# Ten input chunks of a decoder layer's mixer as five pairs with seven block products, and the memory-key projection placed behind the output projection

## The chip, the cores and the metric

The kernel runs on one core of a Trainium2 chip. The metric is the device time of one execution in microseconds (us); the median of three runs of the kernel before is 1890.21 us (1889.72 to 1892.38). The engines are named as the profile names them: PE is TensorE (matmuls), PEld its weight loads, DVE is VectorE, ACT is ScalarE, POOL is GpSimd, and SP issues most of the DMAs. Each engine works through its own instructions in the order in which the built program lists them.

## The reference, cut to what matters

One decoder layer on 256 tokens of width 2048, in float32: a SwiGLU half-step, a mixer, cross-attention into 256 memory tokens, and a second SwiGLU half-step. The change is in the mixer and at the start of the cross-attention.

```python
def hybrid_mixer(h, pos, w_in, ...):
    proj = h @ w_in                       # 2048 -> 6144 + 16 columns
    qa, ka, va, qg, kg, vg, rg, glr = jnp.split(proj, splits, axis=-1)
    qa = rope(rms_norm(heads(qa, 8), attn_q_norm), pos) * (HEAD_DIM ** -0.5)
    ka = rope(rms_norm(heads(ka, 8), attn_k_norm), pos)
    o_attn = dilated_attention(qa, ka, heads(va, 8))
    ...                                   # gated linear attention of qg, kg, vg, glr, gated by silu(rg)
    return jnp.concatenate([o_attn, o_gla], axis=-1) @ w_out

def cross_attention(h, m, ...):
    k = rms_norm((m @ w_k).reshape(...), k_norm)   # m: normed memory tokens
    ...
```

## The kernel before, in words

**Exact products from split operands.** Every float32 operand is split into a high part (a cast) and the rest (operand less high part), and a product is three matmuls: high by high, high by rest, rest by high. The weights are split on the fly. A weight tile `raw` of 128 x 4 x 512 (four k tiles of 128 rows, 512 columns, 1 MB) is loaded by one DMA and split in two halves: ACT casts `wh` (128 x 1024; L157 in `wgroup`, L204 in `parts`) and DVE subtracts for `wl` (L158, L205). There are four buffers each for `wh` and `wl` (`WB`), so a half can be split only when PE is done with an earlier one. The activations lie transposed and split in `xT[0..3]`, four k tiles by 256 tokens each.

**The mixer.** `w_in` has 12 chunks of 512 columns. `proj` takes one chunk: two PSUM banks (one for each block of 128 tokens, t = 0 and 1), four groups of four k tiles, and for each half of a group 12 matmuls of 128x512 (2 token blocks x 2 k tiles x 3), in all 96. The pool `pa` has four banks, so that a chunk's two banks are read while the next chunk fills the other two. The chunks come in the order 6, 7 (queries and keys of the gated linear attention), 8, 9 (its values), 10, 11 (its gates), 0, 2, 1, 3 (attention queries and keys of two head groups), 4, 5 (attention values).

**What follows a chunk** is small work between the splits. For queries and keys (`roped`, L810) it is, for each token block: squares on ACT (L520), their sum on DVE (L522), two small scalings (L525, L526), a power on POOL (L400), the factor on DVE (L530), four scaled copies `un` out of the bank on ACT (L817), and the rotation by a product on POOL (L821), two on DVE (L825) and a sum (L827). Until the last `un` of a token block the bank is held. Turns onto PE (transposes, `scores`, `probs_turn`, `attend`) are put off with `later(n, ...)` by n ticks; a `proj` ticks once for each half of a group. `scores` has, for each of four heads in a group, two reductions with mask (L855), exponentials on ACT (L856), products with counts (L857) and a reciprocal (L860).

**Seven block products.** The two SwiGLU steps already use `seven` (L288): where two column blocks and two groups of four k tiles meet two token blocks, eight products of 128 x 512 x 512 are replaced by seven, with sums of weight tiles and differences of activation blocks (class `Blocks`). A sum of weight tiles is made by DVE (`add`, L211, 128x2048) or by a DMA that POOL issues and that adds into the tile (`add_hbm`, L218). A `product` is 12 matmuls from two halves, so a half feeds six matmuls there; `plain` is the ordinary product for two token blocks and feeds 12 from a half.

**Order.** A list scheduler orders each engine's instructions by priorities (`WPRI`, `LPRI`, `FPRI`) and by its own estimate of when each is ready; pools give out buffers in that order. After the attention values the memory keys are projected (`xattn_w_k`, L967), then the output projection `w_out` runs (L974), then the cross-attention queries.

Of the kernel before, what the change touches and what calls it, by code (L numbers as in the profile page):

```python
# [32 lines left out]
PR0 = 10  # L33
PR1 = 9
ATT = 4
# [5 lines left out]
XPRI = 170  # L41
MEM0 = 2
MEMS = 3
UF = 20
UM = 36
SB = 6
RF = 9
RM = 5


@with_exitstack
def layer_kernel(ctx: ExitStack, tc: tile.TileContext, A: dict, out: bass.AP):
# [48 lines left out]
    def later(n, fn):  # L101
        pend.append([n, fn])
# [67 lines left out]
    def proj(W, c, lhs, groups, fine=None, mid=None):  # L170


        n = W.shape[-1]
        acc = [pa.tile([P, n], F32, tag="acc", name="acc") for _ in range(TT)]
        groups = list(groups)
        for i, g in enumerate(groups):
            if fine and i:
                fine(4 * i)
            if mid and i == 2:
                mid()  # L180
# [107 lines left out]
    def seven(F, ld, rest, hbm):  # L288
# [52 lines left out]
        return Y, Z, R if rest else sv, X  # L341

    def split_from_psum(hi, lo, ps):
        SC.copy(hi, ps)  # L344
        V.tensor_sub(lo, ps, hi.bitcast(F32))  # L345
# [48 lines left out]
    def lhs_x(k, t):  # L394
        hi, lo = xT[k // 4]
        sl = slice(t * P, (t + 1) * P)
        return hi[:, k % 4, sl], lo[:, k % 4, sl]

    def rpow(dst, src):
        G.tensor_tensor(dst, src, mhalf[:, :src.shape[1]], op=ALU.pow)  # L400
# [15 lines left out]
    def ffn(pre, r, after, fine=None, last=False):  # L416
# [3 lines left out]
        def turn(f, hs):  # L420
            for t in range(TT):
# [7 lines left out]
                hT[f, t] = (hi, lo)  # L429

        def x_block(t, c):
            return tuple(p[:, :, t * P:(t + 1) * P] for p in xT[c])

# [35 lines left out]
        for f in range(NF):  # L469
# [34 lines left out]
            if f == 0:  # L504
                up = proj(wu, f, lhs_x, range(4), mid=lambda: F[0].make("22-21", "12-21", "22-12"))
                fill(0, True)
# [111 lines left out]

    def gated(which, c):
        acc = proj(win, c, lhs_x, range(4))  # L620
# [18 lines left out]
    q_turn = gated("q", 6)  # L639

# [45 lines left out]
    later(7, q_turn)  # L686
    k_turn = gated("k", 7)

# [72 lines left out]

    for p2 in range(2):
        acc = proj(win, 8 + p2, lhs_x, range(4))
        for t in range(TT):
            SC.activation(vg[p2][t], acc[t], AF.Copy, scale=r2[:, t:t + 1])
        later(1, lambda p2=p2: states(p2))
        later(3, lambda p2=p2: outputs(p2))

# [12 lines left out]

    for p2 in range(2):
        acc = proj(win, 10 + p2, lhs_x, range(4))
        o2s = []
        for t in range(TT):
# [9 lines left out]
            o2s.append(o2)  # L795
        later(2, lambda p2=p2, o2s=o2s: gate_turn(p2, o2s))

# [11 lines left out]

    def roped(which, g, i, c):  # L810
        acc = proj(win, c, lhs_x, range(4))
        qns = []
# [73 lines left out]

    def values(g):
        acc = proj(win, 4 + g, lhs_x, range(4))
# [12 lines left out]

    roped("q", 0, 0, 0)
    roped("k", 0, 1, 2)
    later(ROPE + SCD, lambda: scores(0, 0))
    later(ROPE + SCD + SCI, lambda: scores(0, 2))
    roped("q", 1, 0, 1)
    later(PR0, lambda: probs_turn(0))
    roped("k", 1, 1, 3)
    later(ROPE + SCD, lambda: scores(1, 0))
    later(ROPE + SCD + SCI, lambda: scores(1, 2))  # L910

# [26 lines left out]
    for c in range(NC):  # L938
        later(MEM0 + MEMS * c, lambda c=c: mem_chunk(c))
    values(0)  # L940
    later(PR1, lambda: probs_turn(1))
    values(1)
    for c in range(NC):
        later(1 + c, lambda c=c: mem_sq(c))

# [20 lines left out]

    acc = proj(A["xattn_w_k"], 0, lhs_mem, range(4))  # L967
    rm = rstd_of(ssm, "rm")
    rmsq = squared(rm, "rmsq")
    heads_T(acc, rm, rmsq, "k", 81, XK)  # L970


    ss3 = new_ss("ss3")
    for c in range(NC):  # L974
        acc = proj(A["w_out"], c, lhs_m, (2, 3, 0, 1))
        for t in range(TT):
            V.tensor_add(xs[c][:, t], acc[t], xs[c][:, t])
        norm_chunk(c, xs[c], 32, ss3)
    r3 = rstd_of(ss3, "r3")
    r3sq = squared(r3, "r3sq")  # L980
# [168 lines left out]
```

## Time and profile before

| | |
|---|---|
| median of 3 runs | 1890.21 us |
| the profiled execution | 1891.93 us, its span (first to last instruction) 1890.2 us |
| mean granted TensorE clock | 0.998 |
| busy in the span: PE, DVE, ACT, POOL | 99%, 81%, 71%, 5% |
| chunks 8 to 5 (five later pairs) | 748.4 to 998.0 us of the span |
| DMA | 433.02 MB, mean 229 GB/s |

The span starts at the first instruction. The timeline gives for each instruction its start, its length and, in brackets, the idle time of its engine before it with what ended it. Instructions of one engine overlap a little (the next starts before the last one's length is over), so what an instruction costs in a row of equal ones is the distance of starts. The stages named below are cut at the times at which ACT starts to read a chunk's bank.

### The profile page before, as it was taken

To read this page: it belongs to the slowest core of one execution; us is meant where nothing else is said; L and a number is where in the kernel's file an instruction comes from. 1 tells how busy PE (TensorE), PEld (TensorE's weight loads), DVE (VectorE), ACT (ScalarE), POOL (GpSimd) and SP (SyncE) were. 2 spreads that over 40 slices of the span, in tenths; PEclk is the share of its full clock that TensorE was granted. 3 is DMA by queue.
4 is the path that set the end of the run, shared out by engine and by line. 5 is a ranking of instruction groups with operands and counts; after the bars stand their busy time and mean duration, and the time that the engine had idled before them with its cause. 6 is when DMAs were issued, how large, how long until landed. Compare 5 with 4: busy or idle time off the path is not lost.

```text
span 1890.2 us, 22717 instructions
## 1 busy us (share of the span) xinstructions
PE 1875.2 (99%) x8552; PEld 1547.0 (82%) x8552; DVE 1527.1 (81%) x1521; ACT 1349.7 (71%) x1785; POOL 90.5 (5%) x103
## 2 busy tenths in 40 slices
PE   9999999999999999999999999999999999999999
PEld 7887888888888888778888889788788888888887
DVE  6989999999999965446775565687999999999994
ACT  6768788787778786445676445566778787878786
POOL 0000000000000000002210000000000000000000
PEclk9999999999999999999999999999999999999999
DMA  9758877987788644445465551756867987788872
GB/s 377 271 199 278 244 229 275 300 250 210 264 286 269 199 184 167 156 156 203 170 223 189 204 186 68 297 176 240 260 207 274 304 252 212 254 284 274 243 235 95
DMA packets 65755, 433.02 MB, mean 229 GB/s; under 512 B 7371, under 2 KB 8523, under 8 KB 14828
## 3 DMA queue, kind: packets, MB, share of 16 engines
q1 hardware_dynamic: 55852, 369.69, 50.8%
q0 software_dynamic: 8064, 58.72, 16.4%
q10 hardware_dynamic: 1728, 3.15, 0.5%
q8 instruction: 67, 1.10, 0.2%
q14 instruction: 44, 0.36, 0.1%
HBM read 429.44 MB, written 2.10 MB: 228 GB/s over the span
## 4 chain that ended last, share of the span: by engine, by line
PE 98%; DVE 1%; DMA 1%; ACT 0%; issue 0%; ACTq 0%
PE acc L231 13%; PE acc L230 13%; PE acc L232 13%; PE acc L167 9%; PE acc L168 9%; PE acc L166 9%; PE dn L166 8%; PE dn L168 8%; PE dn L167 8%; PE tp L426 1%; DMA raw<-in_ffn_w_gate_dram 1%; PE tp L384 0%; DVE wl L205 0%; DVE raw L211 0%; PE dsp L728 0%; PE op L745 0%
## 5 line engine op out<-in xcount | busy, mean ns | idle before, releaser
L205 DVE TENSOR_TENSOR wl<-raw,wh 128x1024 fp32r<-128x1024 f32 x548 | 649.1, 1221 | 93.1 <-ACT wh L204 91.5
L204 ACT CAST wh<-raw 128x1024 fp32r<-128x1024 f32 x548 | 566.2, 1051 | 197.3 <-PE dn L168 84.0
L158 DVE TENSOR_TENSOR wl<-raw,wh 128x1024 fp32r<-128x1024 f32 (+1 forms) x370 | 443.4, 1219 | 182.3 <-ACT wh L157 181.3
L157 ACT CAST wh<-raw 128x1024 fp32r<-128x1024 f32 (+1 forms) x370 | 382.9, 1048 | 199.6 <-PE acc L168 158.4
L166 PE MATMUL dn<-wh,hTh 128*128 128x512 f32 x704 | 274.4, 391 | 0.6 <-ACT hTh L344 0.6
L168 PE MATMUL dn<-wh,hTl 128*128 128x512 f32 x704 | 274.3, 390 | 0.0
L167 PE MATMUL dn<-wl,hTh 128*128 128x512 f32 x704 | 274.2, 389 | 0.0
L231 PE MATMUL acc<-wl,xTh 128*128 128x512 f32 x672 | 263.4, 392 | 2.6 <-DVE wl L205 2.6
L232 PE MATMUL acc<-wh,xTl 128*128 128x512 f32 x672 | 261.8, 390 | 0.0
L230 PE MATMUL acc<-wh,xTh 128*128 128x512 f32 x672 | 261.4, 389 | 0.0
L166 PE MATMUL acc<-wh,xTh 128*128 128x512 f32 x544 | 215.6, 397 | 5.2 <-ACT wh L157 5.2
L211 DVE TENSOR_TENSOR raw<-raw 128x2048 f32<-128x2048 f32 x96 | 218.1, 2286 | 2.6 <-DMA raw<-in_ffn_w_gate_dram 2.5
L167 PE MATMUL acc<-wl,xTh 128*128 128x512 f32 x544 | 213.5, 392 | 0.8 <-DVE wl L158 0.8
L168 PE MATMUL acc<-wh,xTl 128*128 128x512 f32 x544 | 213.2, 392 | 0.0
L230 PE MATMUL acc<-wh,Fh 128*128 128x512 f32 x456 | 179.9, 395 | 0.0
L231 PE MATMUL acc<-wl,Fh 128*128 128x512 f32 x456 | 178.0, 390 | 0.0
L232 PE MATMUL acc<-wh,Fl 128*128 128x512 f32 x456 | 177.6, 389 | 0.0
L166 PEld LDWEIGHTS dn<-wh,hTh 128*128 128x128 f32 x704 | 132.1, 188 | 29.3 <-ACT dn L225 1.2
L168 PEld LDWEIGHTS dn<-wh,hTl 128*128 128x128 f32 x704 | 132.2, 188 | 28.3 <-DVE hTl L345 0.9
L167 PEld LDWEIGHTS dn<-wl,hTh 128*128 128x128 f32 x704 | 132.2, 188 | 27.8 <-DVE wl L158 0.5
L231 PEld LDWEIGHTS acc<-wl,xTh 128*128 128x128 f32 x672 | 126.1, 188 | 33.7 <-DVE wl L205 7.8
L230 PEld LDWEIGHTS acc<-wh,xTh 128*128 128x128 f32 x672 | 126.1, 188 | 26.3
(281 smaller groups left out, 2146.1 us busy)
## 6 DMA issues: line engine op xcount, KB each, us to landing
raw<-in_ffn_w_up_dram SPq DMA_DIRECT2D x88, 1024.0 KB, 9.1
raw<-in_ffn_w_down_dram SPq DMA_DIRECT2D x88, 1024.0 KB, 8.9
raw<-in_ffn_w_gate_dram SPq DMA_DIRECT2D x85, 1024.0 KB, 12.9
raw<-in_ffn_w_gate_dram POOLq DMA_DIRECT2D x56, 1024.0 KB, 8.6
raw<-in_w_in_dram SPq DMA_DIRECT2D x48, 1024.0 KB, 4.8
raw<-in_w_out_dram SPq DMA_DIRECT2D x16, 1024.0 KB, 4.8
raw<-in_xattn_w_k_dram SPq DMA_DIRECT2D x4, 1024.0 KB, 5.1
raw<-in_xattn_w_q_dram SPq DMA_DIRECT2D x4, 1024.0 KB, 4.7
```

What stands on the lines that cost most here:

```text
L157: SC.copy(wh[:, d], src)
L158: splits.append(V.tensor_sub(wl[:, d], src, wh[:, d].bitcast(F32)))
L166: PE.matmul(acc[t], lh, wh, start=first and i == 0, stop=False, **kw)
L167: PE.matmul(acc[t], lh, wl, start=False, stop=False, **kw)
L168: newest[0] = PE.matmul(acc[t], ll, wh, start=False, stop=last and i == len(half) - 1, **kw)
L204: SC.copy(wh, src)
L205: splits.append(V.tensor_sub(wl, src, wh.bitcast(F32)))
L211: V.tensor_add(dst, dst, src)
L230: PE.matmul(bank, hi[:, k], wh, start=start and i == 0, stop=False, skip_group_check=True)
L231: PE.matmul(bank, hi[:, k], wl, start=False, stop=False, skip_group_check=True)
L232: PE.matmul(bank, lo[:, k], wh, start=False, stop=stop and i == len(half) - 1, skip_group_check=True)
L426: PE.transpose(tp[:, j], hs[t][:, j * P:(j + 1) * P], ident)
```

## The change

Chunks 6 and 7 stay as they are. The ten others run as five pairs (c0, c1) = (9, 8), (11, 10), (2, 0), (3, 1), (5, 4). A new generator `pair` takes k groups 0 and 1 of both chunks by seven block products, and groups 2 and 3 by `plain`. Banks Y and Z hold chunk c0's two token blocks, R and X those of c1. `both` interleaves a pair with the next one: R and X are handed out first, then Y's last product follows, then the first product of the next pair, then the rest of Y and Z. The activation differences come from a `Blocks(0)` that is made during chunk 7; two of its five are written over blocks of `xT[0]` and `xT[1]`. The pool of weight tiles grows from 5 to 7 and that of general tiles shrinks from 36 to 28. The loads, sums and splits of the memory tokens and the projection of the memory keys go behind `w_out`. `product` ticks once instead of twice.

```diff
-PR1 = 9
+PR1 = 6
-MEM0 = 2
+MEM0 = 18
-UM = 36
+UM = 28
-RM = 5
+RM = 7
...
         for h, half in enumerate(parts(raw)):
             mms(bank, form, half, start and h == 0, h == 1)
-            tick()
+        tick()
...
+    def pair(F, W, c0, c1, rest):
+        Y, Z = [pa.tile([P, 512], F32, tag="acc", name="acc") for _ in range(2)]
+        T = load(W[c0, 0])
+        add_hbm(T, W[c0, 1])
+        b21 = load(W[c0, 1])
+        yield
+        product(Y, F.A21, T, True)
+        urgent(SC.copy, Z, Y)
+        yield
+        b12 = load(W[c1, 0])
+        add(T, b12)
+        product(Y, F["12-21"], T, False)
+        sw = W2([P, 512], "sw")
+        urgent(SC.copy, sw, Y)
+        product(Z, F["22-21"], b21, False)
+        product(Y, F["21-11"], b12, False)
+        add_hbm(b12, W[c0, 0])
+        sv = W2([P, 512], "sv")
+        urgent(SC.copy, sv, Y)
+        X, R = [pa.tile([P, 512], F32, tag="acc", name="acc") for _ in range(2)]
+        b22 = load(W[c1, 1])
+        add(T, b22)
+        product(R, F.A12, T, True)
+        urgent(V.tensor_sub, X, R, sw)
+        urgent(V.tensor_sub, R, R, sv)
+        forms, g = rest[0]
+        plain((Y, Z), forms, load(W[c0, g]), (1, 0))
+        product(X, F["22-12"], b22, False)
+        for forms, g in rest:
+            plain((R, X), forms, load(W[c1, g]), (0, 1))
+        yield R, X
+        product(Y, F["11-12"], b12, False)
+        yield
+        forms, g = rest[1]
+        plain((Y, Z), forms, load(W[c0, g]), (0, 1))
+        yield Y, Z
...
+    sevens = [pair(Fx, win, c0, c1, rest) for c0, c1 in ((9, 8), (11, 10), (2, 0), (3, 1), (5, 4))]
+    def both(n, out0, out1):
+        out1(next(sevens[n]))
+        if n + 1 < len(sevens):
+            next(sevens[n + 1])
+        next(sevens[n])
+        if n + 1 < len(sevens):
+            next(sevens[n + 1])
+        out0(next(sevens[n]))
...
+    later(4, lambda: Fx.make("22-21", "12-21", "22-12"))
+    next(sevens[0])
+    k_turn = gated("k", proj(win, 7, lhs_x, range(4), mid={3: lambda: next(sevens[0])}))
...
+    both(2, lambda acc: keys(0, acc), lambda acc: queries(0, acc))
+    both(3, lambda acc: keys(1, acc), lambda acc: queries(1, acc))
...
-    acc = proj(A["xattn_w_k"], 0, lhs_mem, range(4))
-    rm = rstd_of(ssm, "rm")
-    ...
     ss3 = new_ss("ss3")
     for c in range(NC):
         acc = proj(A["w_out"], c, lhs_m, (2, 3, 0, 1))
...
+    acc = proj(A["xattn_w_k"], 0, lhs_mem, range(4))
```

How the built programs order this differs at the places where a pair ends. On DVE before, where the queries of chunk 0 leave their banks (`qs`, `qm`, `qf` are the head factors, `t2` and `qn` the rotation, `wl` the splits of the next chunk, each of which feeds 12 matmuls):

```order
L522 TENSOR_REDUCE qs_7156<-sq_7154 128x4
L525 TENSOR_SCALAR qm_7158<-qs_7156,r2sq_5807 128x4
L526 TENSOR_SCALAR qm_7158<-qm_7158 128x4
L530 TENSOR_SCALAR qf_7163<-qr_7161,r2_5792 128x4
L158 TENSOR_TENSOR wl_7255<-raw_7236,wh_7254 128x1024
L825 TENSOR_TENSOR t2_7172<-un_7165,tab_6992 128x4x64 x2
L522 TENSOR_REDUCE qs_7179<-sq_7177 128x4
L827 TENSOR_TENSOR qn_7175<-t1_7170,t2_7172 128x512
L158 TENSOR_TENSOR wl_7273<-raw_7270,wh_7272 128x1024
```

On DVE in the changed kernel, the same queries, where pair (2, 0) ends and pair (3, 1) begins (`raw_7389` is the weight sum T of pair (3, 1)):

```order
L562 TENSOR_REDUCE qs_7343<-sq_7341 128x4
L565 TENSOR_SCALAR qm_7345<-qs_7343,r2sq_5807 128x4
L566 TENSOR_SCALAR qm_7345<-qm_7345 128x4
L570 TENSOR_SCALAR qf_7350<-qr_7348,r2_5792 128x4
L205 TENSOR_TENSOR wl_7425<-raw_7389,wh_7424 128x1024
L211 TENSOR_TENSOR raw_7389<-raw_7389,raw_7515 128x2048
L205 TENSOR_TENSOR wl_7438<-raw_7435,wh_7437 128x1024
L205 TENSOR_TENSOR wl_7454<-raw_7435,wh_7453 128x1024
L205 TENSOR_TENSOR wl_7519<-raw_7389,wh_7518 128x1024
L205 TENSOR_TENSOR wl_7529<-raw_7389,wh_7528 128x1024
L882 TENSOR_TENSOR t2_7359<-un_7352,tab_7100 128x4x64
L205 TENSOR_TENSOR wl_7541<-raw_7392,wh_7540 128x1024
```

One split stood between the factor and the rotation. Now, in the rows shown, a sum of weight tiles and six splits stand behind the factor, with the first half of the rotation among them; a second sum and one more split follow before its other half, and then come the second token block's chain and the keys' chain.

On DVE before, the keys of the second head group, second token block (`ks`, `km`, `kf` as above):

```order
L158 TENSOR_TENSOR wl_7968<-raw_7965,wh_7967 128x1024
L525 TENSOR_SCALAR km_7847<-ks_7845,r2sq_5807 128x4
L526 TENSOR_SCALAR km_7847<-km_7847 128x4
L530 TENSOR_SCALAR kf_7852<-kr_7850,r2_5792 128x4
L158 TENSOR_TENSOR wl_8000<-raw_7965,wh_7999 128x1024
L825 TENSOR_TENSOR t2_7861<-un_7854,tab_6993 128x4x64 x2
L827 TENSOR_TENSOR qn_7864<-t1_7859,t2_7861 128x512
L158 TENSOR_TENSOR wl_8018<-raw_8015,wh_8017 128x1024
```

And in the changed kernel, the same keys where pair (3, 1) ends and pair (5, 4) has begun (`wl_8090` feeds pair (5, 4)'s product into R, `wl_8118` its first plain product):

```order
L562 TENSOR_REDUCE ks_7962<-sq_7960 128x4
L205 TENSOR_TENSOR wl_8090<-raw_7880,wh_8089 128x1024
L565 TENSOR_SCALAR km_7964<-ks_7962,r2sq_5807 128x4
L566 TENSOR_SCALAR km_7964<-km_7964 128x4
L570 TENSOR_SCALAR kf_7969<-kr_7967,r2_5792 128x4
L882 TENSOR_TENSOR t2_7978<-un_7971,tab_7100 128x4x64 x2
L562 TENSOR_REDUCE ks_7985<-sq_7983 128x4
L884 TENSOR_TENSOR qn_7981<-t1_7976,t2_7978 128x512
L565 TENSOR_SCALAR km_7987<-ks_7985,r2sq_5807 128x4
L566 TENSOR_SCALAR km_7987<-km_7987 128x4
L570 TENSOR_SCALAR kf_7992<-kr_7990,r2_5792 128x4
L205 TENSOR_TENSOR wl_8118<-raw_8115,wh_8117 128x1024
```

Two whole chains of head factors, with the first rotation between them, now stand between two splits that PE uses one after the other; before, a split stood within every chain.

More of the change, by code (lines that the diff above doesn't have):

```diff
@@ L616, in layer_kernel, with gated @@
     qeT, keT, kdT = per_t("qeT"), per_t("keT"), per_t("kdT")
-    def gated(which, c):
-        acc = proj(win, c, lhs_x, range(4))
+    def gated(which, acc):
         sc_ = []
@@ L780, in gate_turn, with gates @@
             mT[2 + p2, t] = (hi, lo)
-    for p2 in range(2):
-        acc = proj(win, 10 + p2, lhs_x, range(4))
+    def gates(p2, acc):
         o2s = []
@@ L795, in layer_kernel @@
             o2s.append(o2)
-        later(2, lambda p2=p2, o2s=o2s: gate_turn(p2, o2s))
+        later(2, lambda: gate_turn(p2, o2s))
+    both(1, lambda acc: gates(1, acc), lambda acc: gates(0, acc))
     gb = W2([P, 4, HD], "gb")
@@ L808, in layer_kernel, with roped @@
     pn = {}
-    def roped(which, g, i, c):
-        acc = proj(win, c, lhs_x, range(4))
+    def roped(which, g, i, acc):
         qns = []
@@ L885, in attend, with values @@
             mT[g, "h", h0] = (hi, lo)
-    def values(g):
-        acc = proj(win, 4 + g, lhs_x, range(4))
+    def values(g, acc):
         va = []
```

55 lines of the change are left out of this document (29 added, 26 removed).

## Prediction

> **What bounds the kernel now.** I read the page first: the busy shares and the chain of work that ended last.
>
> ```profile
> PE 1875.2 (99%) x8552; PEld 1547.0 (82%) x8552; DVE 1527.1 (81%) x1521; ACT 1349.7 (71%) x1785; POOL 90.5 (5%) x103
> ...
> PE 98%; DVE 1%; DMA 1%; ACT 0%; issue 0%; ACTq 0%
> ```
>
> PE carries 98% of the chain. A busy PE can hide waits, so I read next what PE itself waited for (line, releaser: us in total, times, longest).
>
> ```profile
> PE acc L166 <- ACT wh L157: 5.2, 3, 3.7
> PE acc L231 <- DVE wl L205: 2.6, 2, 1.3
> PE wps L551 <- DVE x L549: 1.1, 1, 1.1
> PE acc L167 <- DVE wl L158: 0.8, 2, 0.5
> PE dn L166 <- ACT hTh L344: 0.6, 2, 0.3
> PE tp L384 <- DVE xg L386: 0.5, 1, 0.5
> ```
>
> These are all entries: PE loses 10.8 us in the whole span. So PE's matmuls are the time, as long as the splits keep up. Third, the stages: chunks (8, 9), (10, 11), (0, 2), (1, 3), (4, 5) and, last, one round of the first SwiGLU, which runs seven block products already.
>
> ```profile
> core 0: us, PE busy (x) PEld busy (x) DVE busy (x) ACT busy (x) POOL busy (x), PEclk, DMA share, GB/s
> 748.40:802.90 54.50, 54.50 (x257) 43.63 (x256) 26.06 (x29) 24.59 (x35) 1.01 (x1) 1.00 0.48 173
> 802.90:855.00 52.10, 52.10 (x234) 41.28 (x233) 25.30 (x28) 25.21 (x36) 5.08 (x4) 1.00 0.46 163
> 855.00:899.00 44.00, 44.00 (x204) 36.58 (x203) 30.66 (x39) 21.63 (x30) 9.75 (x7) 1.00 0.58 206
> 899.00:950.00 51.00, 51.00 (x239) 42.56 (x238) 39.09 (x82) 33.57 (x62) 11.08 (x9) 1.00 0.48 168
> 950.00:998.00 48.00, 48.00 (x232) 40.39 (x231) 37.94 (x80) 34.97 (x66) 4.01 (x3) 1.00 0.59 207
> ...
> 205.00:266.00 61.00, 61.00 (x274) 50.29 (x273) 56.43 (x48) 48.53 (x59) 2.62 (x3) 1.00 0.80 259
> ```
>
> DVE is half idle in the value and gate chunks, but has 39.1 of 51 us in chunks 1 and 3. The last row will speak for the change: there DVE is busy for 56.4 of 61 us and PE still never waits.
>
> **What goes.** The pace of PE's 128x512 matmuls:
>
> ```profile
> 734.26 0.39 PE L167 MATMUL acc<-wl,xTh 128*128 128x512 f32 x1
> ...
> 743.10 0.39 PE L167 MATMUL acc<-wl,xTh 128*128 128x512 f32 x1
> ```
>
> 39 matmuls lie between these starts: 8.84 / 39 = 0.2267 us each. A pair took 2 x 96 = 192 matmuls and takes 7 x 12 + 96 = 180. Five pairs save 60, **-13.6 us**.
>
> **What comes on DVE.** A pair has 7 + 4 = 11 tiles to split instead of 8, so six more `wl`, two sums of weight tiles and two bank subtractions. The rows for these and for the small work of queries:
>
> ```profile
> 876.07 0.68 DVE L522 TENSOR_REDUCE qs<-sq 128x4 f32<-128x512 f32 x1
> 876.79 0.23 DVE L525 TENSOR_SCALAR qm<-qs,r2sq 128x4 f32<-128x4 f32 x1
> 877.05 0.17 DVE L526 TENSOR_SCALAR qm<-qm 128x4 f32<-128x4 f32 x1
> 878.35 0.23 DVE L530 TENSOR_SCALAR qf<-qr,r 128x4 f32<-128x4 f32 x1 [1.12 <-POOL qr L400]
> 878.48 1.22 DVE L158 TENSOR_TENSOR wl<-raw,wh 128x1024 fp32r<-128x1024 f32 x1
> 879.78 1.87 DVE L825 TENSOR_TENSOR t<-un,tab 128x256 f32<-128x256 f32 x2
> 881.58 0.67 DVE L522 TENSOR_REDUCE qs<-sq 128x4 f32<-128x512 f32 x1
> 882.17 0.68 DVE L827 TENSOR_TENSOR qn<-t,t 128x512 f32<-128x512 f32 x1
> 882.77 1.22 DVE L158 TENSOR_TENSOR wl<-raw,wh 128x1024 fp32r<-128x1024 f32 x1
> ...
> 889.47 3.49 DVE L158 TENSOR_TENSOR wl<-raw,wh 128x1024 fp32r<-128x1024 f32 x3
> ```
>
> ```profile
> 292.85 2.29 DVE L211 TENSOR_TENSOR raw<-raw 128x2048 f32<-128x2048 f32 x1 [0.37 <-DMA raw<-in_ffn_w_gate_dram]
> 295.06 2.35 DVE L205 TENSOR_TENSOR wl<-raw,wh 128x1024 fp32r<-128x1024 f32 x2
> ```
>
> By distance of starts: a split (3.49 - 1.22) / 2 = 1.14, a weight sum 2.21, a 128x512 sum 0.60, one token block's rotation 1.80, and its chain of head factors (876.07 to 878.48) 2.41, of which DVE stands still for 1.12 while POOL takes the power. From the factor to the first rotation lie 1.30 (878.48 to 879.78), here filled by a split. A pair adds 6 x 1.14 + 2 x 2.21 + 2 x 0.60 = 12.5 us. Against the stages above less 12 matmuls (2.7 us), chunks (3, 1) come to 51.6 of 48.3 us: more DVE work than PE has time, before any wait. A half gives PE 12 x 0.2267 = 2.72 us in a plain product but only 1.36 in a block product, and DVE may run ahead by four halves at most. So I walk the three tight places in the new order.
>
> *Place A, chunk 7.* The activation differences (12 operations of 0.60), a weight sum and nine splits lie in one stretch: 7.2 + 2.2 + 10.2 = 19.6 us. PE has 68 matmuls and 8 transposes there:
>
> ```profile
> 898.29 0.87 PE tp L835 x8
> ```
>
> 68 x 0.2267 + 0.87 = 16.3. PE waits for **+3.4** (0 if some of it is ready earlier).
>
> *Place B, pair (2, 0) to (3, 1).* R is full; its queries' chain begins on ACT:
>
> ```profile
> 875.26 0.60 ACT L520 ACTIVATE sq<-acc 128x512 f32<-128x512 f32 x1 [0.36 <-PE acc L168]
> ```
>
> Up to the `wl` that opens the next pair's product into R, DVE has, in order: 0.95 until the squares are there, 10 splits 11.4, two weight sums 4.4, three head chains 7.2, two and a half rotations 4.5, two sums 1.2, and 1.3 where nothing stands between factor and rotation (second block): 31.0 us. PE has 79 matmuls and 8 transposes: 18.8. It waits for 12.2. Behind that, a fourth chain, one and a half rotations, three splits, three sums and a wait of 1.3 (11.6) face 35 matmuls and two transposes (8.1): 3.5 more. Sum **+15.7**. The bound below counts DVE's work alone, as if all its waits were filled: 31.0 - 3 x 1.12 - 1.3 - 0.95 = 25.4, less 18.8 is 6.6. The banks agree: the new pair's Y and Z take the banks of R and X, which are free only after both blocks' `un`; the copy of Y to Z stands on ACT behind them, and PE needs it.
>
> *Place C, pair (3, 1) to (5, 4).* Here the first group's four score heads come in too:
>
> ```profile
> 933.13 0.28 DVE L855 CUSTOM_DVE_ANT_0 s__7619<-sc,off 128x128 f32<-128x128 f32 x1
> ...
> 943.85 0.17 DVE L860 RECIPROCAL rd<-den 128x2 f32<-128x2 f32 x1
> ```
>
> These 10.8 us hold four heads, four splits and a sum: 5.7 for the heads. From the first score to the `wl` of the next pair's first plain half DVE has 14 splits 15.9, two weight sums 4.4, heads 5.7, four chains 9.6, three rotations 5.4, three sums 1.8, and unfilled waits for `un` of 0.2, 1.3 and, as a cast on ACT stands between, 1.9: 46.2. PE has 109 matmuls (24.7) and 2.1 of small work: 26.8. **+19.4**; work alone, 46.2 - 4 x 1.12 - 3.4 = 38.3, gives 11.5.
>
> *The clock.* The longest wait of before shows what an idle PE costs afterwards (in the second fence the granted clock is the third number from the end):
>
> ```profile
> 1199.77 0.73 PE L166 MATMUL acc<-wh,xTh 128*128 128x512 f32 x2 [3.66 <-ACT wh L157]
> ...
> 1203.76 0.63 PE L168 MATMUL acc<-wh,xTl 128*128 128x512 f32 x1
> 1204.18 0.63 PE L166 MATMUL acc<-wh,xTh 128*128 128x512 f32 x1
> ```
>
> ```profile
> 1199.00:1203.00 4.00, 2.70 (x7) 1.88 (x8) 3.75 (x4) 3.67 (x4) 0.00 (x0) 0.67 1.01 426
> 1203.00:1207.00 4.00, 4.00 (x11) 3.13 (x10) 1.60 (x3) 1.04 (x1) 0.00 (x0) 0.50 1.01 426
> ```
>
> After 3.66 us without work the granted clock is 0.50 until about 1207 and a matmul takes 0.427: over 6.5 us that costs 6.5 x (1 - 0.2267 / 0.427) = 3.0. Places B and C together have about five waits of that kind. Much of the slow time falls where PE waits for DVE anyway, so I take **+4** (0 to 15). [...]
>
> *The rest, at nothing.* Ten more loads of 1 MB ride on DMAs that are busy to 46 to 59% in these stages (80% in the SwiGLU row); one that came late would cost its landing of about 5 us once. The banks of values and gates are read by ACT alone, in 0.7 us, under Y's last 12 matmuls (2.7). The memory keys bring the same matmuls; their splits move from a full DVE to the output projection, where it is half idle. If their loads stood in the way of weights there, up to 4 us.
>
> **The sum.** -13.6 + 3.4 + 15.7 + 19.4 + 4 = **+28.9**. On the profiled execution (1891.93) that is 1920.8; it lies 1.7 above the median of its runs (1890.21), so I forecast **1919.1**.
>
> **The rivals.** (1) *DVE keeps up, and the change is faster.* The SwiGLU row speaks for it: 93% DVE and no wait of PE. There DVE does splits and sums only, with nothing that waits for POOL or ACT in a chain; here four such chains stand in a row. It decides if DVE gets through place B in 18.8 us and C in 26.8, against a bare 25.4 and 38.3. Time 1876.6, with place A up to 1880. Chance 0.05; another 0.05 for ending within 0.2% (3.8 us, about what a measurement of this kernel can tell from no change). (2) *Only DVE's work counts, its waits are filled:* -13.6 + 6.6 + 11.5 = +4.5, 1894.7, to 1900 with part of the rest; chance 0.2. Against it: at 878.35 DVE waits although a split stands right behind. [...] (3) *The clock drops in every long wait, exposed:* +15 instead of 4, 1930; chance 0.1. My forecast, 1900 to 1927, has 0.6. The range 1898 to 1934 takes in rival 3 with late loads and most of rival 2.
>
> **What would show it.** Right: PE's matmuls 60 fewer; PE waiting for `wl` (L205), for `wh` and for transposes of `qn`, 30 us or more, nearly all in two stretches of some 40 us at the ends of pairs (2, 0) and (3, 1), with DVE at over 90% or behind POOL there; the granted clock under 1 in them; the gate and value pairs without waits. Wrong: no PE wait over 3 us in the mixer (rival 1); waits of 6 and 11 us with DVE without gaps (rival 2); or waits elsewhere, for DMA or in the output projection.

## The result, and the profile after

| | before | after |
|---|---|---|
| median | 1891.3 us (4 runs, 1889.72 to 1893.38) | 1937.86 us (4 runs, 1936.39 to 1942.04) |
| the profiled execution | 1891.93 us, span 1890.2 | 1938.89 us, span 1937.1 |
| mean granted TensorE clock | 0.998 | 0.989 |

The ratio is 1.0249 (95% interval 1.0229 to 1.0269): 46.6 us slower, where the forecast had 28.9 and a range up to 1934. The engines' totals on the page after:

```profile
PE 1882.7 (97%) x8492; PEld 1543.1 (80%) x8492; DVE 1598.5 (83%) x1585; ACT 1389.4 (72%) x1835; POOL 111.7 (6%) x113
```

The 60 matmuls are gone (8552 to 8492), and yet PE is busy for 7.5 us more. What PE waited for (line, releaser: us in total, times, longest):

```profile
PE acc L230 <- ACT un L874: 8.3, 2, 5.0
PE acc L231 <- DVE wl L205: 6.8, 9, 1.3
PE acc L166 <- ACT wh L157: 6.3, 3, 3.7
PE acc L230 <- ACT acc L225: 6.1, 2, 3.3
PE tp L892 <- DVE qn L884: 4.6, 1, 4.6
PE acc L230 <- ACT wh L204: 3.6, 2, 2.4
PE acc L230 <- ACT Fh L279: 3.6, 2, 2.6
PE tp L835 <- DVE o L849: 3.3, 2, 2.1
...
```

The forecast's names are there (`wl`, `wh`, `qn`), and two that it had only behind them: `un`, the scaled copies out of a bank, and `acc`, the copy of Y that stands on ACT behind them. `Fh`, an activation difference (place A), and `o`, what the gates' transposes read, it did not have as waits. By place, the longest waits in PE's timeline:

```profile
756.96 0.50 PE L230 MATMUL acc<-wh,Fh 128*128 128x512 f32 x1 [2.60 <-ACT Fh L279]
...
885.90 0.44 PE L835 MATMUL tp<-ident,o 128*128 128x128 f32 x2 [2.13 <-DVE o L849]
905.20 1.65 PE L230 MATMUL acc<-wh,xTh 128*128 128x512 f32 x3 [2.37 <-ACT wh L204]
919.80 0.69 PE L892 MATMUL tp<-ident,qn 128*128 128x128 f32 x2 [4.55 <-DVE qn L884]
923.27 0.80 PE L230 MATMUL acc<-wh,Fh 128*128 128x512 f32 x1 [2.78 <-ACT acc L225]
...
978.62 0.50 PE L230 MATMUL acc<-wh,xTh 128*128 128x512 f32 x1 [3.25 <-ACT un L874]
986.12 0.50 PE L230 MATMUL acc<-wh,Fh 128*128 128x512 f32 x1 [3.32 <-ACT acc L225]
999.12 0.79 PE L230 MATMUL acc<-wh,xTh 128*128 128x512 f32 x1 [5.02 <-ACT un L874]
```

With the shorter waits between them, place A (745 to 772) has 7.4 us, the gates' transposes 3.3, place B (905 to 942) 12.9, place C (969 to 1007) 14.5: 38.1 us, of which the kernel before had none. On DVE at place B a weight sum and a split stand ahead of the rotation for whose `qn` PE waits 4.55 us, and the two chains behind it stand without a split between them, as the order showed (DVE ran the rows listed there for the queries in that order, from the reduction `qs` at 899.66 to the sixth split at 913.66):

```profile
914.80 2.28 DVE L211 TENSOR_TENSOR raw<-raw 128x2048 f32<-128x2048 f32 x1
917.00 1.22 DVE L205 TENSOR_TENSOR wl<-raw,wh 128x1024 fp32r<-128x1024 f32 x1
...
919.07 0.68 DVE L884 TENSOR_TENSOR qn<-t,t 128x512 f32<-128x512 f32 x1
...
921.21 0.23 DVE L570 TENSOR_SCALAR qf<-qr,r 128x4 f32<-128x4 f32 x1 [1.12 <-POOL qr L443]
922.65 1.84 DVE L882 TENSOR_TENSOR t<-un,tab 128x256 f32<-128x256 f32 x2 [1.21 <-ACT un L874]
...
927.47 0.23 DVE L570 TENSOR_SCALAR kf<-kr,r 128x4 f32<-128x4 f32 x1 [1.12 <-POOL kr L443]
```

In the first chain DVE waits 1.12 for POOL's power and 1.21 for ACT's copies, and PE stands still until 923.27, for the copy of Y that ACT does behind them; in the second chain DVE waits 1.12 again, while PE works at half speed. Last, the clock at place B, cut at the granted clock's own steps of 3.41 us (the first number after the window is PE's busy time, the third from the end the granted clock):

```profile
901.81:905.22 3.41, 1.04 (x6) 0.54 (x4) 2.23 (x4) 1.63 (x4) 1.37 (x2) 1.00 0.91 380
905.22:908.63 3.41, 3.41 (x8) 2.74 (x9) 3.41 (x2) 1.39 (x3) 2.33 (x1) 0.50 0.02 7
...
918.88:922.29 3.41, 0.69 (x2) 0.29 (x2) 1.41 (x5) 0.81 (x4) 1.01 (x1) 0.50 0.85 295
922.29:925.71 3.42, 2.44 (x6) 1.96 (x7) 2.96 (x4) 1.41 (x4) 1.45 (x1) 0.50 0.03 12
925.71:929.12 3.41, 3.41 (x10) 2.65 (x9) 1.93 (x5) 1.99 (x4) 1.01 (x1) 0.50 0.00 0
```

In the slow stretches that PE works through, 8 to 10 matmuls lie in 3.41 us; at the prediction's 0.2267 it would be 15. Such stretches add up to 30.7 us between 745 and 1012; the kernel before has none there. The time from the last value chunk's reading to the second SwiGLU step is 203.0 us (before: 200.4), so nearly all of the loss lies before it.

### The profile page after: what moved, and what is told of

Same layout as the page of the kernel before. It is cut to its first block, busy times and chain, and to the rows that moved or that the text cites. A ratio compares the mean times of both kernels' runs of the same rounds, so it can differ in the third digit from the quotient of the medians.

```text
span 1937.1 us, 22765 instructions
## 1 busy us (share of the span) xinstructions
PE 1882.7 (97%) x8492; PEld 1543.1 (80%) x8492; DVE 1598.5 (83%) x1585; ACT 1389.4 (72%) x1835; POOL 111.7 (6%) x113
## 4 chain that ended last, share of the span: by engine, by line
PE 54%; DVE 3%; ACT 2%; POOL 1%; issue 1%; ACTq 0%; POOLq 0%
PE acc L230 9%; PE acc L231 9%; PE acc L232 9%; PE dn L166 4%; PE dn L168 4%; PE dn L167 4%; PE acc L166 4%; PE acc L167 4%; PE acc L168 4%; DVE wl L205 1%; ACT wh L204 1%; POOL gsr L845 1%; PE tp L469 0%; ACT un L874 0%; DVE raw L211 0%
## 5 line engine op out<-in xcount | busy, mean ns | idle before, releaser
L205 DVE TENSOR_TENSOR wl<-raw,wh 128x1024 fp32r<-128x1024 f32 x658 | 784.7, 1226 | 133.8 <-ACT wh L204 131.0
L204 ACT CAST wh<-raw 128x1024 fp32r<-128x1024 f32 x658 | 680.7, 1051 | 273.8 <-PE acc L232 99.3
L158 DVE TENSOR_TENSOR wl<-raw,wh 128x1024 fp32r<-128x1024 f32 (+1 forms) x290 | 345.8, 1215 | 117.7 <-ACT wh L157 116.5
L157 ACT CAST wh<-raw 128x1024 fp32r<-128x1024 f32 (+1 forms) x290 | 299.1, 1045 | 125.1 <-PE acc L168 89.3
L230 PE MATMUL acc<-wh,xTh 128*128 128x512 f32 x912 | 360.2, 396 | 15.4 <-ACT un L874 8.3
L231 PE MATMUL acc<-wl,xTh 128*128 128x512 f32 x912 | 360.7, 396 | 6.8 <-DVE wl L205 6.8
L232 PE MATMUL acc<-wh,xTl 128*128 128x512 f32 x912 | 357.7, 392 | 0.0
L232 PEld LDWEIGHTS acc<-wh,xTl 128*128 128x128 f32 x912 | 172.6, 189 | 35.6 <-DVE xTl L280 0.4
L225 ACT ACTIVATE x<-dn 128x512 f32<-128x512 f32 x176 | 105.1, 597 | 38.9 <-PE dn L168 31.5
L230 PEld LDWEIGHTS acc<-wh,Fh 128*128 128x128 f32 x516 | 98.4, 191 | 32.4 <-ACT acc L225 6.7
## 6 DMA issues: line engine op xcount, KB each, us to landing
raw<-in_ffn_w_gate_dram SPq DMA_DIRECT2D x85, 1024.0 KB, 12.9
raw<-in_w_in_dram POOLq DMA_DIRECT2D x10, 1024.0 KB, 10.9
```

Of the source, the lines that this page charges most:

```text
L157: SC.copy(wh[:, d], src)
L158: splits.append(V.tensor_sub(wl[:, d], src, wh[:, d].bitcast(F32)))
L204: SC.copy(wh, src)
L205: splits.append(V.tensor_sub(wl, src, wh.bitcast(F32)))
L225: op(*args, **kw)
L230: PE.matmul(bank, hi[:, k], wh, start=start and i == 0, stop=False, skip_group_check=True)
```

## The experiments

The theory behind the forecast was that DVE's queue, with chains that wait for POOL and ACT, makes PE wait, and that this costs little beyond the waits. Open were how the loss splits over the places, what the clock costs, and whether the order or the amount of DVE's work is the bound.

**1. Only the value and gate pairs.**

```diff
-((9, 8), (11, 10), (2, 0), (3, 1), (5, 4))
+((9, 8), (11, 10))
...
+    Fx.home = {}
...
-    both(2, lambda acc: keys(0, acc), lambda acc: queries(0, acc))
-    both(3, lambda acc: keys(1, acc), lambda acc: queries(1, acc))
+    for g in range(2):
+        queries(g, proj(win, g, lhs_x, range(4)))
+        keys(g, proj(win, 2 + g, lhs_x, range(4)))
...
-    both(4, lambda acc: values(1, acc), first_values)
+    first_values(proj(win, 4, lhs_x, range(4)))
+    values(1, proj(win, 5, lhs_x, range(4)))
```

> Only the value and gate pairs (9, 8) and (11, 10) are left; queries, keys and attention values run as plain chunks again, the activation differences have tiles of their own (7 to 6 weight tiles, 28 to 32 general ones), the memory keys stay behind the output projection. 24 matmuls less are -5.4 us. Forecast on record (place A +3.4, gates nothing): -2.0, so 1889.3 beside 1891.3 for the kernel before. Theory from the changed kernel's trace (waits of 7.4 us in chunk 7 and 3.3 at the gates' transposes, 1.7 of half speed, some 5 us later at the start of chunk 7 and in the tail): +12, 1903. Rival (all of the loss belongs to the three later pairs): 1886 to 1889.

Measured: 1904.3 us, ratio 1.0065 (1.005 to 1.008). So place A and the gates lose by themselves, although 24 matmuls went; the forecast's own 1889 for this part falls. PE's longest waits in it:

```profile
PE acc L230 <- ACT Fh L279: 3.3, 2, 2.6
...
PE tp L836 <- DVE o L850: 2.3, 2, 1.5
PE tp L670 <- ACT qs L663: 2.3, 1, 2.3
```

**2. The memory keys alone.** The kernel before with only this edit; the attention values come ahead of the memory tokens' work, as in the changed kernel.

```diff
-MEM0 = 2
+MEM0 = 18
-UM = 36
+UM = 28
-RM = 5
+RM = 7
...
-        later(1 + c, lambda c=c: mem_sq(c))
+        later(9 + c, lambda c=c: mem_sq(c))
...
-    acc = proj(A["xattn_w_k"], 0, lhs_mem, range(4))
...
     ss3 = new_ss("ss3")
     for c in range(NC):
         acc = proj(A["w_out"], c, lhs_m, (2, 3, 0, 1))
...
+    acc = proj(A["xattn_w_k"], 0, lhs_mem, range(4))
```

> The kernel before with nothing but the memory keys put behind the output projection, with their ticks, 7 weight tiles and 28 general tiles as in the changed kernel. Forecast on record (at nothing, up to +4): 1891 to 1895. Theory that the pairs carry the loss: 1891.3 within 2. Rival (chunk 7 starts 2.4 us later in the changed kernel and the tail is 2.5 longer, and both belong to this move): 1896.

Measured: 1892.1 us, ratio 1.0004 (0.9995 to 1.0014). The move costs nothing; the forecast's "at nothing" holds, and the pairs carry the loss.

**3. Waits filled with idle matmuls.** `hold(n)` issues n matmuls of 128x512 whose result nothing reads.

```diff
+        if c0 in (3, 5):
+            hold(12)
         product(Y, F.A21, T, True)
         urgent(SC.copy, Z, Y)
         yield
+        if c0 in (3, 5):
+            hold(12)
...
+        if c0 == 5:
+            hold(12)
         product(R, F.A12, T, True)
```

> The changed kernel with 12 idle matmuls (2.7 us) put ahead of each place where PE waits at the start of pairs (3, 1) and (5, 4): ahead of the first product into Y, ahead of the product that reads Y's copy, and in the last pair ahead of the product into R; 60 in all. They lie in time that PE waits for ACT or DVE anyway. Theory (a wait of over 2.4 us halves the clock for 3.4 to 10 us, and this slow time costs about 9 us of the loss at these places): the granted clock stays at 1.00 at most of these places, 1930 to 1934 beside 1937.9. Rival (slow time is hidden behind DVE, the clock costs no more than the 4 us forecast): 1936 to 1940. If the idle matmuls stand in the way themselves: up to 1951.

Measured: 1932.2 us (1930.7 to 1934.1; ratio to before 1.0211, 1.0196 to 1.0227): 5.7 us faster than the changed kernel with 60 matmuls more to do. PE's busy time and the granted clock from 745 to 1012, first in the changed kernel, then here:

```profile
745.00:1012.00 267.00, 228.69 (x967) 177.09 (x968) 206.00 (x260) 153.38 (x224) 52.10 (x35) 0.94 0.56 178
```

```profile
745.00:1012.00 267.00, 241.56 (x1045) 188.70 (x1046) 206.49 (x260) 158.60 (x232) 53.95 (x35) 0.97 0.57 181
```

The half speed falls from 30.7 to 17.1 us; 5.7 / 13.6 is 0.42 us for each us of it. PE's idle time in the stretch falls by 12.9 us, which is about what the idle matmuls fill (60 x 0.2267 = 13.6): waits and filling together are as long as the waits were. The clock is a cost of its own, and not hidden behind DVE.

**4. Banks copied out at once.**

```diff
+        held = []
+        for t in range(TT):
+            h_ = U([P, 512], F32, "held")
+            urgent(SC.copy, h_, acc[t])
+            held.append(h_)
+        acc = held
         for t in range(TT):
             f = head_scale(acc[t], r2, r2sq, t, which == "q", 1.0, which)
```

> The changed kernel, but the two banks of each query and key chunk are copied at once by ACT into tiles of SBUF, from which head factors and scaling then read; eight copies of 0.6 us on ACT. Theory A (PE waits because banks are held until the last scaled copy, 8.3 us for un and 6.1 for the copy of Y behind it): these waits go with some 6 us of half speed, 1915 to 1925. Theory B (DVE's chains and splits in order are what is late, the held banks only show it): the waits come back under wl, wh and qn, 1932 to 1942.

Measured: 1938.1 us, ratio to before 1.0246 (1.0229 to 1.0263): no gain. The waits for `un` are gone, and as many stand under other names (39.7 us in all from 745 to 1012, 38.1 in the changed kernel):

```profile
PE tp L898 <- DVE qn L890: 12.0, 2, 7.3
PE acc L230 <- ACT sw L225: 8.0, 2, 5.0
```

So the held banks only show what is late; freeing them does not help as long as the rotation that the transposes need is as late (7.3 us at its worst).

**5. Activation differences and gates.**

```diff
+    Fx.make("22-21", "12-21", "22-12")
...
-    later(4, lambda: Fx.make("22-21", "12-21", "22-12"))
...
-        later(2, lambda: gate_turn(p2, o2s))
+        later(4, lambda: gate_turn(p2, o2s))
```

> The changed kernel with the three first activation differences made right behind chunk 6 instead of in the middle of chunk 7, where DVE is busy for only 3 to 5 of 10 us, and the gates' transposes 4 instead of 2 ticks behind their chunk. Theory (place A and the gates are each a local pile of work in order, 7.4 and 3.3 us of waits and 1.3 to 1.7 of half speed): all but 1 to 3 us of it goes, 1926 to 1930 beside 1937.9. Rival (DVE is full over the whole stretch, so the waits only move to wl and the pair that follows): 1935 to 1940.

Measured: 1927.1 us, ratio to before 1.0192 (1.0178 to 1.0206): 10.8 us less with the edits at these two places. Neither `Fh` nor `o` is among PE's waits any more, though a wait of 2.75 us for `wl` has come up at 862.4; the waits of places B and C are about as long as they were (28.2 us, 27.4 in the changed kernel):

```profile
PE acc L231 <- DVE wl L205: 9.4, 10, 2.7
PE acc L230 <- ACT un L874: 9.2, 2, 6.0
```

**6. Other pairs, and both edits.** A pair of one heavy and one light chunk has two chains at its end instead of four.

```diff
-((9, 8), (11, 10), (2, 0), (3, 1), (5, 4))
+((0, 8), (2, 9), (1, 10), (3, 11), (5, 4))
...
-    both(0, lambda acc: gated_values(1, acc), lambda acc: gated_values(0, acc))
...
-    both(1, lambda acc: gates(1, acc), lambda acc: gates(0, acc))
...
-    both(2, lambda acc: keys(0, acc), lambda acc: queries(0, acc))
-    both(3, lambda acc: keys(1, acc), lambda acc: queries(1, acc))
+    both(0, lambda acc: queries(0, acc), lambda acc: gated_values(0, acc))
+    both(1, lambda acc: keys(0, acc), lambda acc: gated_values(1, acc))
+    both(2, lambda acc: queries(1, acc), lambda acc: gates(0, acc))
+    both(3, lambda acc: keys(1, acc), lambda acc: gates(1, acc))
```

> The changed kernel with the ten chunks paired otherwise, (0, 8), (2, 9), (1, 10), (3, 11), (5, 4), so that each of four pairs has one chunk of queries or keys and one of values or gates; the number of matmuls, splits, sums and chains is the same. At a pair's end two head chains stand in a row instead of four, and the banks handed out first are read by ACT alone. Theory (the loss at places B and C is chains of two chunks back to back on DVE's queue, with the banks held behind them, and the clock after the waits; some 27 us of waits and 11 of half speed): more than two thirds of it goes, 1900 to 1912. Rival (DVE's work alone, 12.5 us more a pair than before, is what PE waits for): the work is the same, so 1925 to 1940.

> Both edits together: pairs (0, 8), (2, 9), (1, 10), (3, 11), (5, 4), activation differences made right behind chunk 6, gates' transposes 4 ticks behind. Theory: the gains add up, 1890 to 1902, against 1891.3 for the kernel before; below 1891.3 only if what is left of waits and half speed is under the 13.6 us of the saved matmuls. Rival (gains do not add, since DVE is full over the whole stretch): 1908 to 1925.

Measured: 1934.8 us (ratio 1.0238, 1.0222 to 1.0253), and with the edits of experiment 5 1929.2 (1.0203, 1.0189 to 1.0216). The second lies above theory and rival alike: the two edits gain 5.7 us on these pairs where experiment 5 alone gained 10.8. My theory that chains back to back are the loss falls: the waits for `un` are even longer (13.8 and 14.4 us, 8.3 in the changed kernel). What stands where in the first of the two, on ACT, on DVE and on PE:

```profile
931.59 0.59 ACT L560 ACTIVATE sq<-acc 128x512 f32<-128x512 f32 x1
```

```profile
932.01 1.22 DVE L205 TENSOR_TENSOR wl<-raw,wh 128x1024 fp32r<-128x1024 f32 x1
933.14 2.28 DVE L211 TENSOR_TENSOR raw<-raw 128x2048 f32<-128x2048 f32 x1
935.35 5.76 DVE L205 TENSOR_TENSOR wl<-raw,wh 128x1024 fp32r<-128x1024 f32 x5
...
942.22 0.67 DVE L562 TENSOR_REDUCE qs<-sq 128x4 f32<-128x512 f32 x1
```

```profile
946.04 0.80 PE L230 MATMUL acc<-wh,xTh 128*128 128x512 f32 x1 [7.40 <-ACT un L872]
```

The squares are there at 932.2, but the first step of the chain that frees the bank comes at 942.2, behind a weight sum and six splits, PE standing still from 938.6. Two of these splits are for the very product that PE can't begin until the bank is free: it runs from 946.0 on, and DVE makes no split between 941.0 and 952.6.

**7. Order or work.** On the kernel of experiment 5, one run changes the order alone (both blocks' head factors together, with the copies out of the bank, ahead of the splits), one the work alone (no weight sums in the three later pairs); a third has the new order with the mixed pairs.

```diff
+        with tc.high_priority(FPRI):
+            fs = [head_scale(acc[t], r2, r2sq, t, which == "q", 1.0, which) for t in range(TT)]
...
-            f = head_scale(acc[t], r2, r2sq, t, which == "q", 1.0, which)
+            f = fs[t]
...
-                SC.activation(un[:, h]..., scale=f[:, h:h + 1])
+                urgent(SC.activation, un[:, h]..., scale=f[:, h:h + 1])
```

```diff
-        add(T, b12)
+        if c0 > 6:
+            add(T, b12)
...
-        add(T, b22)
+        if c0 > 6:
+            add(T, b22)
```

> The kernel with early activation differences (1927.1 us), and in the three later pairs the head factors of both token blocks together, with the scaled copies out of the bank, at a priority above the weight splits. The work is the same, its order on DVE and ACT is not. Theory P (a bank is held by a chain that DVE's queue has behind splits of the very products that wait for the bank): the waits for un (9.2) and for the copy of Y (4.9) go in great part, with half speed behind them, 1908 to 1918. Rival W (DVE has more work than PE has time, in whatever order): the waits come back under wl and wh, 1922 to 1930.

> The kernel with early activation differences (1927.1 us), less the six weight sums on DVE in the three later pairs (6 x 2.21 = 13.3 us of DVE): two products of each of these pairs take the tile unsummed, so attention queries, keys and values come out otherwise. Theory W (DVE's work is the bound there): 13 us and some half speed go, 1909 to 1914. Theory P (the order of chains and splits is): less than half of that, 1920 to 1926.

> Pairs (0, 8), (2, 9), (1, 10), (3, 11), (5, 4) with early activation differences (1929.2 us), and the head factors and scaled copies first, as in the run before. There 14.4 us of waits for un stand at the ends of the third and fourth pair, where DVE had splits of products ahead of the chain that holds their banks. Theory P: these go, 1905 to 1914. Rival W: 1922 to 1930, under wl and wh.

Measured: order 1921.2 us (ratio 1.0162, 1.0147 to 1.0177), 5.9 less than experiment 5; work 1916.4 (1.0139, 1.0122 to 1.0155), 10.7 less for 13.3 us of DVE; order with mixed pairs 1915.9 (1.0135, 1.012 to 1.015), 13.2 less than the mixed pairs with both edits. All three lie between what theory P and rival W expected: both count. With the mixed pairs the order takes most of the waits for `un` away (14.4 to 4.0 us), puts 9.4 us for `qn` in their place and leaves `wl`; PE's waits from 745 to 1012 fall from 32.9 to 24.5 us:

```profile
PE acc L231 <- DVE wl L205: 10.2, 9, 2.3
PE tp L892 <- DVE qn L884: 9.4, 3, 4.2
...
PE acc L230 <- ACT un L225: 4.0, 2, 2.8
```

With the pairs as they were, theory P is right about the copy of Y (4.9 to 0.7 us) and wrong about `un`: 8.8 us of it stay (9.2 before), in four waits instead of two, the longest 3.3 instead of 6.0. The missing work takes waits for `wl` (9.4 to 5.6), `qn` (4.6 to none) and `un` (9.2 to 0.7) and leaves those for copies that stand behind chains:

```profile
PE acc L230 <- ACT acc L225: 8.5, 2, 4.3
PE acc L230 <- ACT sw L225: 6.0, 2, 3.3
```

**8. The light pairs mended.** The kernel of experiment 1 with the edits of 5; then its gated keys' turns later; then ACT's reading of chunks 6 and 7 ahead of its casts.

```diff
-    later(1, k_turn)
-    later(3, gated_scores)
-    later(4, kd_turn)
+    later(3, k_turn)
+    later(5, gated_scores)
+    later(7, kd_turn)
```

```diff
-            SC.activation(qs, acc[t], AF.Copy, scale=...)
+            urgent(SC.activation, qs, acc[t], AF.Copy, scale=...)
```

> Only the value and gate pairs, as in the run that had 1904.3, with the activation differences right behind chunk 6 and the gates' transposes 4 ticks behind their chunk. In that run the waits of chunk 7 were 8.5 us, the half speed there 4.6, the gates' transposes 1.5. Theory: these go, 24 matmuls less are left of the change, 1888 to 1892. Rival (the waits move to wl): 1898 to 1904.

> The kernel of value and gate pairs with early activation differences (1893.0 us), and the turns of the gated keys put two and three ticks later (transposes of qs 1 to 3, scores 3 to 5, kd 4 to 7). In the run before PE waits there 1.7 us for qs and 2.0 for keT, and the clock stands at 0.5 for 6.8 us behind them. Theory (two small waits close together are enough for half speed; without them 24 matmuls less, 5.4 us, are left of the change): 1885.5 to 1888.5, below the kernel before (1890.8). Rival (the waits move on to the next instruction that needs DVE, and the clock drops all the same): 1891 to 1894.

> The kernel of value and gate pairs with the later turns (1892.7 us), and ACT's reading of the banks of chunks 6 and 7 at a priority above the weight casts, so that the transposes of qs find their data. There PE waited 1.7 us for qs and 0.8 for Fl, and the clock stood at 0.5 for 6.8 us. Theory (these waits are all that is left in the way): 1.7 + 0.8 us and some 2.5 to 3 of half speed go, 1886.5 to 1889 beside 1890.7 for the kernel before. Rival (the clock drops again behind another wait): 1890.5 to 1893.

Measured: 1893.0 us (ratio 1.001, 1.0001 to 1.0019), 1892.7 (1.001, 1.0001 to 1.0019) and 1887.7 (0.998, 0.9972 to 0.9989). The first lies 1.0 above what its theory expected, and the second was a miss: PE's wait for `qs` of 1.7 us stayed, since ACT reads that bank late whatever the turn's tick, and with it 6.8 us of half speed. When ACT reads first, both are gone: from 700 to 1012 us PE waits once, for 0.7 us. The kernel before has no wait of PE there, so this last edit has nothing to gain in it. This version is faster than both kernels, by 3.3 us beside the kernel before; 24 matmuls less are worth 5.4.

**9. The price of a wait by itself.** The kernel before with a wait of known length in the middle of each of the chunks 8, 9, 10, 11.

```diff
+    def stall(n):
+        d = W2([P, 512], "d")
+        urgent(V.memset, d, 0.0)
+        one = PM([P, P], "one")
+        PE.matmul(one, ident, ident, start=True, stop=True)
+        urgent(V.tensor_copy, d[:, 0:P], one)
+        for i in range(n):
+            urgent(V.tensor_copy, d, d)
+        two = PM([P, P], "two")
+        return PE.matmul(two, d[:, 0:P], ident, start=True, stop=True)
...
+            end = stall(still) if still and i == 2 else None
...
+                with tc.issue_after(end.ins) if end and h == 0 else nullcontext():
```

> The kernel before with four waits of PE put in on purpose, one in the middle of each of the chunks 8, 9, 10, 11, where PE otherwise never waits: a matmul of 128x128, on DVE a copy of it and two copies of 128x512 one behind the other, and a matmul that reads the last; PE's matmuls that follow stand behind it. By a 128x512 sum's 0.60 us each wait is some 1.5 to 2.5 us. Theory (a wait of that length costs half speed for 3.4 us or more behind it, 1.4 to 3 us each): the time rises by the waits and 6 to 12 us more. Rival (the forecast's price, 4 us for five events): the waits and 3 us more. Third case (waits under 2.4 us leave the clock alone): the waits alone, 6 to 10.

> The same with seven copies, so that each of the four waits is some 4 to 5 us. Theory: the time rises by the four waits and 1.5 to 3.2 us each for half speed, 6 to 13 us more than the waits. Rival (the forecast's price, 0.8 us for an event): the waits and 3 us.

Measured: 1901.9 us (ratio 1.0056, 1.0042 to 1.007) and 1924.7 (1.0177, 1.0163 to 1.019). The long waits are 4.6 to 4.8 us each, 18.8 in all, and the gates' transposes wait 1.0 more; the time rises by 33.8, so each costs another 3.5. One of them, in steps of 3.41 us:

```profile
799.22:802.63 3.41, 0.00 (x0) 0.00 (x0) 3.27 (x7) 0.76 (x1) 0.00 (x0) 1.00 0.07 19
802.63:806.04 3.41, 2.30 (x6) 1.91 (x7) 0.99 (x3) 0.00 (x0) 0.00 (x0) 0.50 0.74 288
806.04:809.45 3.41, 3.41 (x9) 2.64 (x8) 0.00 (x0) 0.00 (x0) 0.00 (x0) 0.50 0.00 0
809.45:812.87 3.42, 3.42 (x16) 2.82 (x15) 1.23 (x1) 1.50 (x2) 0.00 (x0) 1.00 0.00 0
```

DVE makes the last of its copies at the start of the slow stretch and does nothing more until 809.45: nothing else is late. Each of the four has 6.8 us at half speed. Of the short waits (2.5, 1.3, 1.3 and 1.4 us), the first alone brings half speed, for 3.41 us; the others leave the clock at 1.00:

```profile
763.98:767.40 3.42, 0.91 (x8) 0.74 (x7) 2.28 (x4) 2.21 (x4) 0.00 (x0) 1.00 0.22 38
767.40:770.82 3.42, 3.42 (x10) 2.65 (x9) 0.00 (x0) 0.00 (x0) 0.00 (x0) 0.50 0.64 268
798.12:801.53 3.41, 2.10 (x11) 1.66 (x11) 2.28 (x4) 1.04 (x1) 0.16 (x1) 1.00 0.00 0
801.53:804.95 3.42, 3.42 (x16) 2.81 (x16) 0.71 (x1) 1.05 (x1) 0.00 (x0) 1.00 0.80 295
```

The long waits rise above the short ones by 22.9 us, of which 12.3 are the waits; the other 10.6 belong to 23.9 us more of half speed (27.3 against 3.4): 0.44 us for each, as in experiment 3 (0.42). For the long waits the theory holds, with 3.5 a little over its 3.2, and the forecast's 0.8 for an event does not. For the short ones it misses: the time rises by 10.9 us, 7.5 of them waits (1.0 at the gates' transposes here too), and the other 3.4 are under its 6 to 12. They lie by the rival's 3, but not for its reason: one event, not four, slowed the clock, and its 3.41 us are worth about 1.5 at 0.44. No row names the rest.

## Why the prediction was wrong

The direction, the mechanism and places A, B and C were right; the gates as a place were missed, and the size was off: +46.6 instead of +28.9.

- *Matmuls, -13.6.* Right: 60 fewer.
- *Waits, 3.4 + 15.7 + 19.4 = 38.5.* The sum came out at 38.1, but as 7.4 at A, 3.3 at the gates, 12.9 at B, 14.5 at C: that it agrees is luck, since errors cancel. 27.4 of it lie at the ends of the two pairs, where the forecast had nearly all. A was too small, because it set all of DVE's work against all of PE's, while PE stops at the first difference (`Fh`, 2.60 us) and not at the end of the pile. The gates were set at nothing because only the reading of their banks was counted, not the transposes of `o`, which stand on PE two ticks behind. Experiment 5, with its edits at both, gave 10.8 us back.
- *The clock, +4: the step that failed.* "About five waits of that kind" at B and C were forecast, and five stretches of half speed came there (a sixth stands at A); at the forecast's 3.0 each that is 15. What failed is the step from 15 to 4, that "much of the slow time falls where PE waits for DVE anyway": of the 30.7 us at half speed PE worked in 25.3 and stood still in 5.4. At place B it is busy for 3.41, 2.44 and 3.41 us in three of the four slow stretches shown, doing half. At 0.42 to 0.44 (experiments 3 and 9) the 30.7 us are **13 us**, 9 more than forecast. Waits of 2.4 us brought half speed too, which nothing before showed. The forecast's upper end for this term, 15, and rival 3 with 1930 had it. At B and C, the forecast for waits and clock together (15.7 + 19.4 + 4 = 39.1) comes out as measured (27.4, and 11.7 for 27.3 us of half speed at 0.43), as if slow time and waits could be exchanged; experiment 3 speaks against that, because there the time fell when the clock stayed up, with waits and filling as long as before.
- *The rest, at nothing.* The memory keys cost nothing (experiment 2), and PE waits for no DMA in the mixer. Banks of values and gates: no wait.
- *Rival 2, only DVE's work counts:* not as it was put, since the unfilled waits are there (1.12 and 1.21 in the rows above). But work counts beside order: 13.3 us less of it gave 10.7 (experiment 7).
- *What no term had:* -13.6 + 38.1 + 13 is 37.5; 9 us are left. 2.4 of them lie ahead of chunk 7 in the profiled execution (its start is at 720.3 instead of 717.9), a place whose time differs from run to run of these kernels by 3.5 us. About 4 more belong to the waits: a listed wait begins at the recorded end of the matmul before it, 0.39 us behind its start, but PE's pace is 0.2267. By the distance of starts the 22 waits from 745 to 1012 cost 42.4 us beyond that pace, not 38.1. Another 2 lie in the matmul that follows the first one behind a wait: at full speed it starts 0.15 late on average. What is left is under 1 us.

## What to carry to other kernels

Where an engine that feeds PE is near its limit, price a wait of PE as its length and, on top, what the clock cost here: 3.5 us behind each wait of 4.6 to 4.8 us and, as an estimate, 1.5 behind the one of 2.5 (3.41 us of half speed at 0.44 each), while behind those of 1.3 to 1.4 it stayed at 1.00 (experiment 9); don't let the one hide in the other. Seven products instead of eight paid here only where the feeding engine had room for the additional splits and sums: the pairs of values and gates (DVE half idle) gained 3.3 us once every wait was gone, and the pairs of queries and keys (DVE at three quarters) lost in every order tried. Work that frees a bank should stand ahead of work for the product that wants the bank; that gave 13.2 us with the mixed pairs, and 5.9 with the others.

## What the runs showed of the hardware

*The granted clock changed in steps of 3.41 us.* In the traces of all 17 kernels, from 700 to 1260 us, I divided the time at the steps of the granted clock and added up PE's idle time in each. Of the stretches at full speed, 2600 had less than 1.68 us of idle time, and none was followed by half speed; 64 had more than 1.92, and all were; of nine in between, six were. From half speed the clock came back after all 68 stretches with less than 0.32 us of idle time, and after none of 43 with more than 0.55; of five in between, after two. The traces of the two kernels compared here have 317 of the stretches at full speed: 309 with at most 1.71 us of idle time, none followed by half speed, and eight with 2.00 or more, all followed by it. In these runs half speed went with the sum of the idle times in a stretch, not with the length of one: in the changed kernel waits of 1.25 and 0.76 us (ended at 1005.73 and 1006.99) lie in one stretch, and half speed follows at 1007.62; its wait of 3.25 us (ended at 978.62), divided by a step (1.54 and 1.71), left the clock at 1.00. In the second version of experiment 8 a wait of 1.72 us with one of 0.29 beside it had half speed behind it.

*A DVE product that started while POOL's product ran took longer.* In the first run of experiment 6, the same product of 128x128, without and with a product on POOL beside it, on DVE and on POOL:

```profile
914.38 0.29 DVE L912 SCALAR_TENSOR_TENSOR pc<-p__7387,cnt 128x128 f32<-128x128 f32 x1 [0.62 <-ACT p__7387 L911]
...
925.34 1.39 DVE L912 SCALAR_TENSOR_TENSOR pc<-p__7441,cnt 128x128 f32<-128x128 f32 x1
```

```profile
924.98 2.90 POOL L844 TENSOR_TENSOR gsr<-sr,gon 128x512 f32<-128x512 f32 x2 [28.85 <-ACT sr L842]
```

0.29 us become 1.39. In the changed kernel the two halves of a rotation took 1.84 us with POOL's product beside them (at 922.65, above; the first half starts just before POOL's product, the second behind its start), and without it:

```profile
988.82 0.75 DVE L882 TENSOR_TENSOR t<-un,tab 128x256 f32<-128x256 f32 x2
```

Which of the two started first made the difference: in the 17 traces all 129 DVE products of 128x256 that started while a 128x512 product ran on POOL took 1.49 to 1.53 us, and the 100 that had started before POOL's took at most 0.49 (in the two kernels compared here 15 took 1.50 to 1.53 and 13 at most 0.48). The kernel before has the same pairing (1.87 us in the prediction's rows), and DVE loses some 11 us by it from 745 to 1045 us before as after, so it explains little of the difference; no run here took it away.
